# Seven half-width products for the second matmul, and loads that cast, in a two-matmul ReGLU block

## Chip, cores, metric

One core of a Trainium2 chip. The metric is device time in microseconds (us) of one launch. Three executions of the kernel before took 335.81, 336.21 and 337.5 us; the median is 336.21.

## The reference

```python
x  : [16, 256, 512]  -> 4096 rows of 512, float32
w1 : [512, 4096]        w2 : [2048, 512]
h = x @ w1
gate, value = np.split(h, 2, axis=-1)
h = np.maximum(gate, 0) * value
return (h @ w2).astype(np.float32)
```

## The kernel before, in words

All matmuls run in float16 with float32 sums. The 4096 rows are cut into four **stages** (s = 0 to 3) of 1024 rows. A stage has a block phase (the first matmul and the gating) and a second-matmul phase.

**Block phase.** The first matmul is a 2x2 block product. Its row halves are the two groups of 512 rows of the stage, its inner halves the two halves of the 512 columns of x, its column halves gate and value. It is done in seven products instead of eight, on sums of blocks: of x (tiles `x_A11` to `x_A22`, sums `x_S1` to `x_S4`) and of w1 (tiles `w_B11`, `w_B21`, `w_B22` and the sums `w_T1` to `w_T4`). One `Block(jb)` makes 128 gate and 128 value columns; there are 16 in a stage (in stage 0 the blocks 0 and 1 are done plainly, class `Plain`, while w1 still comes in). Each product P1 to P7 of a block is two matmuls of 128x128 by 128x512.

The order is written out by hand in **slots**: block jb places its products at `jb * 7` plus 0, 1, 3, 4, 5, 9, 13 for P1, P5, P2, P6, P3, P7, P4, so that the seven slots of a period are filled by two blocks. Within a block P1 goes to a PSUM bank X, ScalarE copies X to a bank Y (L228), and only then may P2 add to X and P6 to Y. ScalarE also takes W (L235) and Y (L242) out; VectorE makes the gated result `g` with four operations per block (L248, L249, L254, L258).

**Second-matmul phase.** `mm2_stream(s, g)` (L281) yields one matmul at a time: for each of eight 128-row groups it adds up 16 matmuls of 128x128 by 128x512 (L286) in one bank; ScalarE scales the result out (L298), and the sync queue SP stores it. `advance(stream, n)` takes n of them. Ten of them fill free slots at the end of the blocks, four (`TAIL`) the free slots of the next stage's first block.

**Inputs.** w1 comes in as float32 pieces through a staging tile (L195, SP); GpSimd makes the four sums (L203 to L206) and ScalarE three casts (L207). The first 1024 rows of x come in as float32 and are turned by TensorE (L358), later ones are cast by ScalarE (L186) and turned by VectorE in 32x32 blocks (L189). `x_sums` (L158, VectorE) makes S1 to S4. w2 is loaded by GpSimd's queue with a cast (L461).

**Looks.** The kernel also checks that the mean square of each piece of its inputs is in a range, and else runs a general path that is not used here. A look at 1024 columns of w1 or w2 is a squaring with a sum on ScalarE (`look_whole`, L173); the looks at later x are folds on GpSimd (`look`, L164 to L168). `LOOKS` says at which block each is issued, after that block's P6. Before, w1 is looked at in the 16 blocks of stage 1 and w2 in the first 8 blocks of stage 2, one look a block.

All engines' orders are those of the program text (`manual_schedule`); the waits between them are put in by the framework.

Of the kernel before, what the change touches and what calls it, by code (L numbers as in the profile page):

```python
# [16 lines left out]
P = 128  # L17
TH = 512
PERIOD = 7
NWARM = 30  # L20
# [3 lines left out]
SLOT = {"P1": 0, "P5": 1, "P2": 3, "P6": 4, "P3": 5, "P7": 9, "P4": 13}  # L24

# [71 lines left out]
def fast_way(ctx, tc, x2, w1, w2, out2, flag):  # L97

# [4 lines left out]
    NS = T // (2 * TH)  # L109
    NJ = H // P  # L110
    NB = 2 * TH // P
# [3 lines left out]
    xpool = ctx.enter_context(tc.tile_pool(name="xpool", bufs=2))  # L115
    gpool = ctx.enter_context(tc.tile_pool(name="gpool", bufs=1))
    stage = ctx.enter_context(tc.tile_pool(name="stage", bufs=3))
    halfs = ctx.enter_context(tc.tile_pool(name="halfs", bufs=4))
    tmp = ctx.enter_context(tc.tile_pool(name="tmp", bufs=4))
    psx = ctx.enter_context(tc.tile_pool(name="psx", bufs=3, space=bass.MemoryType.PSUM))  # L120
    psy = ctx.enter_context(tc.tile_pool(name="psy", bufs=3, space=bass.MemoryType.PSUM))
    psw = ctx.enter_context(tc.tile_pool(name="psw", bufs=2, space=bass.MemoryType.PSUM))

    x_v = x2.rearrange("(s h tb r) (q c) -> s h q r tb c", h=2, tb=16, r=32, q=4)
    w1_v = w1.rearrange("(p e) (g j) -> p (e g) j", e=4, g=2)
    w2_v = w2.rearrange("(hc p) n -> p hc n", p=P)
    out_v = out2.rearrange("(s b p) n -> s b p n", p=P, b=NB)

    wop = {n: wpool.tile([P, 2, H], F16, name=f"w_{n}") for n in ("B11", "B21", "B22", "T1", "T2", "T3", "T4")}
    w2_sb = wpool.tile([P, NJ, DO], F16, name="w2_sb")
    w_stage = wpool.tile([P, 4, 1024], F32, name="w_stage")
    g_set = {0: gpool.tile([P, NJ, 2 * TH], F16, name="g", tag="g")}

    NX = 8 + (NS - 1) * 32
    st = wpool.tile([P, NX + 16 + NJ // 2], F32, name="st")


# [3 lines left out]
    ident = wpool.tile([P, P], F32, name="ident")  # L143
    for i in range(NWARM):
        pool, nm = (psy, "Y") if i < 16 else (psx, "X")
        t = pool.tile([P, TH], F32, name=nm, tag=nm)
        n = TH if i < 16 else TH // 2
        nc.tensor.matmul(t[:, :n], warm_b[:, :P], warm_b[:, :n], start=True, stop=True)


    def x_tiles():
        return {n: xpool.tile([P, 2, TH], F16, name=f"x_{n}", tag=f"x_{n}")
                for n in ("A11", "A12", "A21", "A22", "S1", "S2", "S3", "S4")}

    def x_sums(o):
        for n, i0, i1, op in (("S1", "A21", "A22", ADD), ("S2", "S1", "A11", SUB), ("S4", "A12", "S2", SUB),
                              ("S3", "A11", "A21", SUB)):
            yield nc.vector.tensor_tensor(o[n], o[i0], o[i1], op=op)  # L158

    def look(t, at):  # L160

        n, m = t.shape[1:]
        fold = tmp.tile([P, n, m], F32, name="fold", tag="fold", bufs=1)
        nc.gpsimd.tensor_tensor(fold, t, t, op=MULT)  # L164
        while m > 2:
            m //= 2
            nc.gpsimd.tensor_tensor(fold[:, :, :m], fold[:, :, :m], fold[:, :, m:2 * m], op=ADD)  # L167
        nc.gpsimd.tensor_tensor(st[:, at:at + n], fold[:, :, 0], fold[:, :, 1], op=ADD)  # L168

    def look_whole(t, at, of, half=False):  # L170

        sq = tmp.tile([P, 1024], F16, name="sq", tag="sq", bufs=1)
        nc.scalar.activation(sq[:, :of], t, SQUARE, scale=(P / of / (2 if half else 1)) ** 0.5,  # L173
                             accum_out=st[:, at:at + 1])

    def load_x(s, i):

        t = stage.tile([P, 8, P], F32, name="xs", tag="xs")
        for q in range(4):
            nc.sync.dma_start(out=t[q * 32:(q + 1) * 32], in_=x_v[s, i // 2, q, :, i % 2 * 8:i % 2 * 8 + 8])  # L180
        return t

    def turn_x(o, t, i):
        ts = slice(i % 2 * 256, i % 2 * 256 + 256)
        c = halfs.tile([P, 8, P], F16, name="xh", tag="xh")
        nc.scalar.copy(out=c, in_=t)  # L186
        halves.append(c)
        for k in range(2):
            nc.vector.transpose(o[f"A{i // 2 + 1}{k + 1}"][:, :, ts].rearrange("p b (tb r) -> p b tb r", r=32),  # L189
                                c.rearrange("p tb (c k b) -> p k b tb c", k=2, b=2)[:, k])  # L190


    def load_w1(eng, jb, n, u):
        t = w_stage[:, u:u + n].rearrange("p u v -> p (u v)").rearrange("p (eg j) -> p eg j", eg=8)
        eng.dma_start(out=t, in_=w1_v[:, :, jb * P:(jb + n) * P])  # L195
        return t.rearrange("p (k b g) j -> p k b g j", k=2, b=2)

    def w1_ops(jb, n, t):

        js = slice(jb * P, (jb + n) * P)  # L200
        b11, b21, b12, b22 = t[:, 0, :, 0], t[:, 1, :, 0], t[:, 0, :, 1], t[:, 1, :, 1]
        op = {n: w[:, :, js] for n, w in wop.items()}
        nc.gpsimd.tensor_tensor(op["T1"], b12, b11, op=SUB)  # L203
        nc.gpsimd.tensor_tensor(op["T2"], b22, (op["T1"]), op=SUB)
        nc.gpsimd.tensor_tensor(op["T3"], b22, b12, op=SUB)
        nc.gpsimd.tensor_tensor(op["T4"], b21, (op["T2"]), op=SUB)  # L206
        return [lambda o=o, i=i: nc.scalar.copy(out=o, in_=i)  # L207
                for o, i in ((op["B11"], b11), (op["B21"], b21), (op["B22"], b22))]

# [4 lines left out]
    class Block:  # L214
# [3 lines left out]
        def mm(self, name, ps, fresh):  # L218
            wn, xn = WX[name]
            for b in range(2):  # L220
                nc.tensor.matmul(ps, wop[wn][:, b, self.jb * P:(self.jb + 1) * P], self.xo[xn][:, b, :],  # L221
                                 start=fresh and b == 0, stop=b == 1, skip_group_check=True)
# [38 lines left out]
    class Plain:  # L261


# [3 lines left out]
        def products(self, h, a1, a2):  # L267
            js = slice(self.jb * P, (self.jb + 1) * P)
            X = psx.tile([P, TH], F32, name="X", tag="X")
            W = psw.tile([P, TH], F32, name="W", tag="W")  # L270
            for a, gate, value in ((a1, "B11", "T3"), (a2, "B21", "B22")):
                for ps, wn in ((X, gate), (W, value)):
                    for b in range(2):
                        nc.tensor.matmul(ps, wop[wn][:, b, js], a[:, b, :], start=a is a1 and b == 0,
                                         stop=a is a2 and b == 1)
            v = tmp.tile([P, 2, TH], F32, name="v", tag="tmp")[:, 0]
            nc.scalar.activation(v, W, COPY, scale=GS)
# [3 lines left out]
    def mm2_stream(s, g):  # L281
        last = s == NS - 1
        for b in range(NB):
            ps = psx.tile([P, DO], F32, name="O", tag="X")
            for hc in range(NJ):
                nc.tensor.matmul(ps, g[:, hc, b * P:(b + 1) * P], w2_sb[:, hc, :],  # L286
                                 start=hc == 0, stop=hc == NJ - 1)
                if hc < NJ - 1:
                    yield
            o = tmp.tile([P, DO], F32, name="o", tag="tmp")  # L290
            if last and b == NB - 1:
                h = DO // 2
                nc.scalar.activation(o[:, :h], ps[:, :h], COPY, scale=1 / GS)  # L293
                nc.scalar.dma_start(out=out_v[s, b, :, :h], in_=o[:, :h])
                nc.vector.tensor_scalar(out=o[:, h:], in0=ps[:, h:], scalar1=1 / GS, scalar2=None, op0=MULT)  # L295
                nc.sync.dma_start(out=out_v[s, b, :, h:], in_=o[:, h:])
            else:
                nc.scalar.activation(o, ps, COPY, scale=1 / GS)  # L298
                nc.sync.dma_start(out=out_v[s, b], in_=o)
            yield  # L300

# [4 lines left out]


    wl = [(0, 1, 0), (1, 1, 1)] + [(jb, 2, jb % 4) for jb in range(2, NJ, 2)]
    ws, copies = {}, []

    def fetch(i, eng):
        if i < len(wl):
            assert not copies
            jb, n, u = wl[i]
            ws[i] = load_w1(eng, jb, n, u)

    def prepare(i):
        jb, n, _ = wl[i]
        copies.extend(w1_ops(jb, n, ws.pop(i)))

    def copy_some(n):
        for c in copies[:n]:
            c()
        del copies[:n]

    def plain_w(i):
        jb, n, _ = wl[i]
        t = ws.pop(i)
        js = slice(jb * P, (jb + n) * P)
        nc.scalar.copy(out=wop["B11"][:, :, js], in_=t[:, 0, :, 0])  # L330
        nc.gpsimd.tensor_copy(out=wop["T3"][:, :, js], in_=t[:, 0, :, 1])
        nc.gpsimd.tensor_copy(out=wop["B21"][:, :, js], in_=t[:, 1, :, 0])
        nc.scalar.copy(out=wop["B22"][:, :, js], in_=t[:, 1, :, 1])

    def plain_w_end(jb, n):
        js = slice(jb * P, (jb + n) * P)
        op = {n: w[:, :, js] for n, w in wop.items()}
        nc.gpsimd.tensor_tensor(op["T1"], op["T3"], op["B11"], op=SUB)
        nc.gpsimd.tensor_tensor(op["T2"], op["B22"], op["T1"], op=SUB)
# [184 lines left out]
```

## Time and profile before

| what | value |
|---|---|
| timed executions | 335.81, 336.21, 337.5 us |
| profiled execution, first to last instruction (span) | 334.7 us |
| median less span, what lies around it | 1.5 us |
| first block product of stages 0, 1, 2, 3 starts at | 20.78, 93.07, 172.74, 251.05 us |
| last matmul starts at | 328.41 us |
| TensorE matmul busy | 321.7 us |
| VectorE, ScalarE, GpSimd busy | 199.5, 180.6, 113.1 us |
| mean granted TensorE clock | 0.997 |

The device time of the profiled execution itself isn't listed; what lies around the span is taken as the 1.5 us above. The starts of the stages are read in the timeline as the first matmul of block 0 (in stage 0 of block 2). A matmul's listed duration is its latency with a modelled end (379 ns for 512 columns); what it costs in a row of matmuls is the distance between starts, 0.216 us.

### The profile page before, as it was taken

Reading aid. Unit: us, or ns where it says so; the run is one execution under the profiler, and the core shown is the slowest. Engines: PE = TensorE matmul, PEld = TensorE weight load, DVE = VectorE, ACT = ScalarE, POOL = GpSimd, SP = SyncE. Lnnn points to the kernel's source line nnn. Section 1 sums busy time; section 2 is a strip of 40 time slices with the busy share of each in tenths; the row PEclk is TensorE's granted clock in tenths of the full one; section 3 lists DMA queues with packets and bytes.
Section 4 is the critical chain, followed back from the end, with each engine's and each line's share of the span. In section 5 each row is a group of like instructions: output and inputs, shape, how many; then the busy total and the mean of one; then the engine's idle time right before and its main releaser. Section 6 shows DMA issues by size and latency. Waiting matters only on the chain. (4 is left out here: it accounts for less than half of the span.)

```text
span 334.7 us, 4222 instructions
## 1 busy us (share of the span) xinstructions
PE 321.7 (96%) x1475; PEld 145.0 (43%) x1475; DVE 199.5 (60%) x307; ACT 180.6 (54%) x332; POOL 113.1 (34%) x142
## 2 busy tenths in 40 slices
PE   8979999999999999999999999999999999999992
PEld 4634444444444444444443444444444444444441
DVE  0477888866038778775207788885805888882000
ACT  2568798832267878764128785554215555541120
POOL 1679979299800000038950000019970000000000
PEclk9999999999999999999999999999999999999998
DMA  8946599942126000004116300004120000000212
GB/s 252 358 144 182 195 238 161 169 113 78 63 90 163 1 0 0 2 1 158 65 63 162 58 2 0 0 2 125 63 96 31 1 1 2 0 0 33 94 65 69
DMA packets 30458, 27.59 MB, mean 82 GB/s; under 512 B 1632, under 2 KB 25440, under 8 KB 30432
## 3 DMA queue, kind: packets, MB, share of 16 engines
q1 hardware_dynamic: 27136, 24.52, 24.8%
q0 software_dynamic: 2112, 2.10, 3.9%
q10 hardware_dynamic: 1184, 0.66, 0.6%
q8 instruction: 13, 0.21, 0.3%
q14 instruction: 13, 0.11, 0.1%
HBM read 20.97 MB, written 8.39 MB: 88 GB/s over the span
## 5 line engine op out<-in xcount | busy, mean ns | idle before, releaser
L286 PE MATMUL O<-w_sb,g 128*128 128x512 f16 x512 | 113.4, 379 | 0.0
L248 DVE SCALAR_TENSOR_TENSOR cc<-W,pu 128x512 f32<-128x512 f32 x62 | 42.9, 692 | 73.3 <-ACT pu L242 73.2
L286 PEld LDWEIGHTS <-g 128*128 128x128 f16 x512 | 50.1, 98 | 60.5 <-issue 0.2
L164 POOL TENSOR_TENSOR fold<-xh 128x1024 f32<-128x1024 f16 x12 | 24.0, 1999 | 114.0 <-ACT xh L186 113.3
L298 ACT ACTIVATE o<-O 128x512 f32<-128x512 f32 x31 | 18.5, 597 | 69.1 <-PE O L286 65.3
L242 ACT ACTIVATE pu<-Y 128x512 f32<-128x512 f32 x62 | 37.0, 597 | 33.6 <-PE Y L221 32.7
L228 ACT COPY Y<-X 128x512 f32<-128x512 f32 x62 | 35.9, 578 | 25.1 <-PE X L221 17.9
L249 DVE SCALAR_TENSOR_TENSOR g<-X,cc 128x512 f16<-128x512 f32 x62 | 42.9, 692 | 2.3
L258 DVE SCALAR_TENSOR_TENSOR g<-Y,cc 128x512 f16<-128x512 f32 x62 | 42.3, 681 | 2.7 <-PE Y L221 2.7
L167 POOL TENSOR_TENSOR fold<-fold 128x512 f32<-128x512 f32 (+2 forms) x72 | 41.3, 574 | 5.6
L254 DVE SCALAR_TENSOR_TENSOR cc<-Y,pu 128x512 f32<-128x512 f32 x62 | 42.3, 682 | 0.1
L235 ACT ACTIVATE pu<-W 128x512 f32<-128x512 f32 x62 | 37.1, 598 | 0.0
L221 PEld LDWEIGHTS <-w_B_89 128*128 128x128 f16 x124 | 12.1, 97 | 23.3 <-issue 12.0
L221 PEld LDWEIGHTS <-w_T_94 128*128 128x128 f16 x124 | 12.1, 97 | 15.8 <-issue 3.5
L221 PEld LDWEIGHTS <-w_T_93 128*128 128x128 f16 x124 | 12.1, 98 | 14.6
L221 PEld LDWEIGHTS <-w_T_91 128*128 128x128 f16 x124 | 12.1, 98 | 14.6
L221 PEld LDWEIGHTS <-w_B_88 128*128 128x128 f16 x124 | 12.0, 97 | 14.7
L221 PEld LDWEIGHTS <-w_T_92 128*128 128x128 f16 x124 | 12.0, 97 | 14.7
L221 PEld LDWEIGHTS <-w_B_90 128*128 128x128 f16 x124 | 12.0, 98 | 14.4
L295 DVE TENSOR_SCALAR o<-O 128x256 f32<-128x256 f32 x1 | 0.4, 425 | 25.3 <-ACT o L293 25.3
L186 ACT CAST xh<-xs 128x1024 f16<-128x1024 f32 x12 | 12.2, 1042 | 5.4 <-DMA xs<-in_x_dram 5.4
L203 POOL TENSOR_TENSOR w_T_91<-w_stage 128x512 f16<-128x512 f32 x7 | 9.2, 1313 | 7.5 <-DMA w_stage<-in_w_dram 7.3
(155 smaller groups left out, 429.9 us busy)
## 6 DMA issues: line engine op xcount, KB each, us to landing
out_dram<-o SPq DMA_DIRECT2D x31, 256.0 KB, 2.0
w_stage<-in_w_dram SPq DMA_DIRECT2D x7, 1024.0 KB, 6.9
xs<-in_x_dram SPq DMA_DIRECT2D x48, 128.0 KB, 3.9
w_sb<-in_w_dram POOLq DMA_DIRECT2D x4, 512.0 KB, 8.6
w_stage<-in_w_dram ACTq DMA_DIRECT2D x1, 512.0 KB, 5.3
w_stage<-in_w_dram SPq DMA_DIRECT2D x1, 512.0 KB, 6.6
x_A_162<-in_x_dram SPq DMA_DIRECT2D x1, 256.0 KB, 2.8
x_A_163<-in_x_dram SPq DMA_DIRECT2D x1, 256.0 KB, 4.1
```

The costliest lines, as they stand in the source:

```text
L164: nc.gpsimd.tensor_tensor(fold, t, t, op=MULT)
L167: nc.gpsimd.tensor_tensor(fold[:, :, :m], fold[:, :, :m], fold[:, :, m:2 * m], op=ADD)
L221: nc.tensor.matmul(ps, wop[wn][:, b, self.jb * P:(self.jb + 1) * P], self.xo[xn][:, b, :], start=fresh and b == 0, stop=b == 1, skip_group ...
L228: nc.scalar.copy(out=self.Y, in_=self.X)
L235: nc.scalar.activation(self.p5, self.W, COPY, scale=GS)
L242: nc.scalar.activation(self.u2, self.Y, COPY, scale=GS)
L248: nc.vector.scalar_tensor_tensor(out=self.c12, in0=self.W, scalar=GS, in1=self.u2, op0=MULT, op1=ADD)
L249: nc.vector.scalar_tensor_tensor(out=self.g[:, self.jb, :TH], in0=self.X, scalar=0.0, in1=self.c12, op0=MAX, op1=MULT)
L254: nc.vector.scalar_tensor_tensor(out=self.c22, in0=self.Y, scalar=GS, in1=self.p5, op0=MULT, op1=ADD)
L258: nc.vector.scalar_tensor_tensor(out=self.g[:, self.jb, TH:], in0=self.Y, scalar=0.0, in1=self.c22, op0=MAX, op1=MULT)
L286: nc.tensor.matmul(ps, g[:, hc, b * P:(b + 1) * P], w2_sb[:, hc, :], start=hc == 0, stop=hc == NJ - 1)
L298: nc.scalar.activation(o, ps, COPY, scale=1 / GS)
```

## The change

- **Second matmul.** The products of g and w2 get the same seven-product scheme: row halves of 512 rows, inner halves of 8 chunks of 128 (`NHC`), column halves of 256 (`HALF`). Per stage and 128-row group b (now 0 to 3) there are seven products of 8 matmuls with 256 columns, so 224 matmuls of 256 columns a stage instead of 128 of 512. `advance` takes 4 at a time where it took 2.
- **Sums of g.** Stages 1 to 3: GpSimd sums S3 block by block for blocks 0 to 7, and S1, S2, S4 for blocks 8 to 13, after each block's P4; VectorE does S1, S2, S4 of the last two (`BY_DVE`). Stage 0: VectorE does all, in eight operations of 2048 columns after the last block.
- **Sums of w2** (`w2_ops`): four GpSimd operations of 2048 columns, issued at block 14 of stage 0.
- **w1 and the first x** are cast by loading DMAs on GpSimd's queue; the ScalarE casts and the staging tile go. `fetch_more` issues the rest of w1, w2 and the casts of later x from there, three fetches each at blocks 2, 4 and 6.
- **Later x** is cast from DRAM to DRAM (`x16`), turned by four transposing DMAs on SP per stage, and read again as rows (`fetch_rows`) for the looks. `xpool` has one buffer where it had two.
- **Looks** at x go to ScalarE, 256 columns each, sixteen a stage; those at w1 to blocks 8 to 15 of stages 1 and 2; those at w2 to blocks 1 to 8 of stage 3.
- 10 warming matmuls where there were 30, and 8 filling ones between the first turn and the first products.

```diff
-    w1_v = w1.rearrange("(p e) (g j) -> p (e g) j", e=4, g=2)
+    w1_v = w1.rearrange("(e p) (g j) -> p e g j", p=P, g=2)
+    def w1_ops(i):
+        turned(lambda n, a, b, o: nc.gpsimd.tensor_tensor(W[n](i), W[a](i), W[b](i), op=o))
+    def w2_ops():
+        turned(lambda n, a, b, o: nc.gpsimd.tensor_tensor(V[n], V[a], V[b], op=o))
...
-    def mm2_stream(s, g):
+    def mm2_stream(s, go):
+        def mm(name, b, ps, fresh):
+            vn, gn = WX[name]
+            for k in range(NHC):
+                nc.tensor.matmul(ps, go[gn][:, k, b * P:(b + 1) * P], V[vn][:, k, :], start=fresh and k == 0,
+                                 stop=k == NHC - 1, skip_group_check=True)
...
+            if name == "P1":
+                d["X"] = take(psx, "X")
+                yield from mm("P1", b, d["X"], True)
+                d["Y"] = take(psy, "Y")
+                nc.scalar.copy(out=d["Y"], in_=d["X"])
...
+        for b in range(0, NB, 2):
+            for name in ("P1", "P2", "P5", "P6", "P3", "P7", "P4"):
+                for c in (b, b + 1):
+                    yield from step(name, c)
...
+    for b in range(0, NB, 2):
+        nc.gpsimd.dma_start(out=xn[:, b:b + 2], in_=x_v[0, :, b:b + 2])
+    fetch_w1(0)
+    make_identity(nc, ident)
+    nc.gpsimd.dma_start(out=xn[:, NB:], in_=x_v[0, :, NB:])
+    for i in range(1, 6):
+        fetch_w1(i)
...
+    for s in range(NS):
+        for i in range(4 * NB):
+            at_block(s, (4 if s == 0 else i // (2 * NB)) + i // 2, lambda s=s, i=i: look_x(s, i))
+    for i in range(2 * NP):
+        at_block(1 + i // NP, 8 + i % NP, lambda i=i: look_w1(i))
+    for i in range(NJ // 2):
+        at_block(3, 1 + i, lambda i=i: look_w2(i))
...
                 if s == 0 and n == "P5" and jb % 2 == 0:
+                    for _ in range(3):
+                        fetch_more(queued)
+                        queued += 1
+                    if jb // 2 + 1 < NP:
+                        w1_ops(jb // 2 + 1)
+                    else:
+                        w2_ops()
+                        w1_ops(0)
                 getattr(blocks[jb], n)()
+                if n == "P1" and s and jb == 4:
+                    xn = fetch_rows(s, 1)
...
+                if n == "P4" and s:
+                    if jb < NHC:
+                        g_sum(nc.gpsimd, go, "S3", jb, jb + 1)
+                    elif jb < NJ - BY_DVE:
+                        for m in ("S1", "S2", "S4"):
+                            g_sum(nc.gpsimd, go, m, jb - NHC, jb - NHC + 1)
...
+        if s == 0:
+            for m in ("S1", "S2", "S4", "S3"):
+                for h in (0, NHC // 2):
+                    g_sum(nc.vector, go, m, h, h + NHC // 2)
+        else:
+            for m in ("S1", "S2", "S4"):
+                g_sum(nc.vector, go, m, NHC - BY_DVE, NHC)
...
+            for h in range(2):
+                for k in range(2):
+                    nc.sync.dma_start_transpose(out=xo[f"A{h + 1}{k + 1}"],
+                                                in_=x16[s + 1][h * TH:(h + 1) * TH, k * 256:k * 256 + 256])
+            xn = fetch_rows(s + 1, 0)
+            advance(stream, 100)
```

## The prediction

> **What bounds the kernel now.** I read the page's engine sums first, then its groups, then the timeline.
>
> ```profile
> PE 321.7 (96%) x1475; PEld 145.0 (43%) x1475; DVE 199.5 (60%) x307; ACT 180.6 (54%) x332; POOL 113.1 (34%) x142
> L286 PE MATMUL O<-w_sb,g 128*128 128x512 f16 x512 | 113.4, 379 | 0.0
> ```
>
> TensorE is busy from end to end, and the second matmul waits for nothing (0.0). So the end is set by TensorE's work plus what it waits for in the blocks. The price of a narrower matmul is in the timeline at the start:
>
> ```profile
> 6.75 1.69 PE L148 MATMUL X<-warm 128*128 128x256 f16 x14
> 8.28 0.72 PE L358 MATMUL W<-ident,x_A_162 128*128 128x128 f32 x4
> ```
>
> 14 matmuls of 256 columns, each with its own weight load, take 8.28 - 6.75 = 1.53 us: 0.1093 us each. Those of L286 start 0.2157 us apart. Weight loads are 0.098 us, so they just hide at 256 columns.
>
> The blocks are bound by a chain through ScalarE (ACT). The timeline of a block of stage 1:
>
> ```profile
> 105.61 0.60 ACT L242 ACTIVATE pu<-Y 128x512 f32<-128x512 f32 x1 [0.59 <-PE Y L221]
> 106.11 1.05 ACT L173 ACTIVATE sq<-w_B_88 128x1024 f16<-128x1024 f16 x1
> 107.06 0.19 ACT L173 ACTIVATION_READ_ACCUMULATOR sq<-w_B_88 128x1 f32 x1
> 107.15 0.59 ACT L228 COPY Y<-X 128x512 f32<-128x512 f32 x1
> 107.66 0.59 ACT L235 ACTIVATE pu<-W 128x512 f32<-128x512 f32 x1
> 108.85 0.60 ACT L242 ACTIVATE pu<-Y 128x512 f32<-128x512 f32 x1 [0.59 <-PE Y L221]
> ...
> 257.81 0.57 ACT L228 COPY Y<-X 128x512 f32<-128x512 f32 x1 [0.70 <-PE X L221]
> ```
>
> See two things. From the copy L228 to the next L242 is 1.70 us, then 0.50 us, then the look (1.04 us), then the next copy: a period of 3.23 us. Without a look (stage 3, last line) ACT idles 0.70 us and the period is 3.03, TensorE's own 14 x 0.2157. So a look has 0.7 to 0.8 us to hide in, and its excess is on the path.
>
> Last, GpSimd (POOL) and VectorE (DVE) together:
>
> ```profile
> 79.67 2.34 POOL L164 TENSOR_TENSOR fold<-xh 128x1024 f32<-128x1024 f16 x1
> 80.17 2.38 DVE L158 TENSOR_TENSOR x_S_788<-x_A_782,x_A_784 128x1024 f16<-128x1024 f16 x1
> 82.08 1.60 POOL L167 TENSOR_TENSOR fold<-fold 128x512 f32<-128x512 f32 x1
> ```
>
> The same sum takes 0.69 us elsewhere. Here it ends at 82.55, 0.54 after GpSimd's operation (82.01), and GpSimd's next one is then late: they take turns, one whole instruction each.
>
> **What the Trainium skill says.** "TensorE: Matmul & The Clock Gate", Back-to-back issue gap: N/2.4 + 2.5 ns, so 109 and 216 ns; the trace agrees. Its Part 1 says that about 3.4 us of idleness halves the clock; the warming matmuls agree from the other side (0.427 us apart at first, 0.216 later). "SBUF — State Buffer", Who interferes with whom: a VectorE instruction with two SBUF inputs and a GpSimd instruction that reads SBUF exclude each other; the lines above agree. "DMA: Bandwidth & Descriptors", Latency and other measured facts: transposing DMAs reach 261 GB/s; nothing in this trace shows one.
>
> **The change, part by part.** The reckoning is against the profiled span, 334.7 us; the median is 1.5 above it, which I add at the end.
>
> *Second matmul.* 512 x 0.2157 = 110.4 us becomes 4 x 224 x 0.1093 = 97.9: **-12.5 us**, 3.1 a stage, all on the path. Its copies: P1's X to Y (256 columns, about 0.37 us by the 384 ns of L293) lies under the other group's 8 matmuls (0.87 us); that cover is thin (0.2 us) but is not taken by other work. P4 waits likewise for a VectorE operation of 0.43 us (L295). I cost both at nothing, at most 0.2 us x 32 = 6.
>
> *Start.* The first block product starts at 20.78. GpSimd's casting loads (L461: 0.76 us to issue, first packet 1.65 us after the issue, 4.2 MB in 11.9 us, so 2.97 us a MB) bring half of x by 5.7, the first w1 by 9, the rest of x by 12, the next w1 pair by 15. Turning in float16, two plain blocks (6.9 us) and the copies between give a first block at 18.9: -1.9. In stage 0 ACT's casts go (periods of 3.65, 3.66 and 3.3 shrink towards 3.05), -1.5.
>
> *GpSimd in stage 0.* Its queue does not wait for TensorE, only for data and itself: 15 issues x 0.76 end at 12.9; from 15.3 (data) on 7 x 4.65 for `w1_ops` (L338 to L341: 1.16 each) and 11 issues x 0.76 = 8.4. So `w2_ops` starts at 56.3. Blocks 6 and 8 wait 0.8 us for their sums meanwhile. A sum of w2 has 2048 columns: 0.2 us plus 2048 x 1.87 ns (from 1.16 at 512 and L168's 0.2) is 4.0 us; the four end at 60, 64, 68, 72, then `w1_ops(0)` to 77. The DRAM-to-DRAM issues aren't shown; 0.5 to 2 us each (three), I take 0.76.
>
> *End of stage 0.* With these, the last P4 is at t = 65.4 (before: 68.04). VectorE then owes eight sums of 2048 columns, 1.1 us each (0.54 for 1024 once let in). From 66.7 they take turns with GpSimd's remaining operations (4.0, 4.0, then four of 1.15): S1 is whole at 74.3, S2 78.8, S4 83.3, S3 85.6. TensorE wants S1 at 67.1 (12 x 0.1093 after P4) and each next 16 matmuls (1.75 us) later, so it follows: P7 at 85.7. Then 136 matmuls to stage 1's first block: 14.9 us, so 100.6, plus about 2 because a wait of 7 us lets the clock fall: **102.6 against 93.07, +9.5**. Without the turns it would be 90.7.
>
> *Looks.* A look of 256 columns is 0.31 + 0.09 = 0.40 us (from 0.95 at 1024 and 0.52 at 512). Two in a block, 0.80, fit in. One at w, 1.04, costs 0.2 as before. Both together: 1.70 + 0.49 + 1.84 = 4.03, so +1.0. That is block 8 of stages 1 and 2, and blocks 1, 2, 3, 5, 6, 7, 8 of stage 3: 7 x 1.0 there, where ACT had no look before.
>
> *Stages 1 to 3.* 224 x (0.2157 + 0.1093) = 72.8 us of work. Waits: 0.4 at the first block (as shown before), 1.0 + 7 x 0.2 for looks, 0.4 for S1 of the last two blocks (P4's result, then 0.69 us on VectorE). Stage 1: 76.0 (was 79.67), stage 2: 76.0 (78.31). Stage 3 to the last matmul: 72.8 + 0.4 + 7.0 + 0.2 + 0.4 = 80.8 (77.57). Sum -3.7 - 2.3 + 3.2 = **-2.8**. GpSimd's sums of g (six blocks x 3 x 1.14 = 20.5 us beside 3.03 to 3.23 a block) end within a microsecond of the last P4, just not late; VectorE's block operations have one SBUF input and share nothing.
>
> *Later x.* The ACT casts and VectorE turns lay under the second matmul: nothing saved. The four transposing DMAs stand on SP ahead of `fetch_rows` and of the output stores. They wait for the last block to free its x tiles (one buffer now). By the skill's 261 GB/s they take 1 us each; they have some 15 us before VectorE's sums fall late, so up to about 4 us each costs nothing, 8 us each some 10 us a stage. I take nothing. The stores behind them have four result tiles.
>
> *Tail.* Narrower last pieces: -0.2.
>
> Sum: 334.7 + 9.5 - 2.8 - 0.2 = 341.2; with 1.5 around it, **342.7, say 342.5**.
>
> **Rivals.**
> A, faster. GpSimd gets through `w2_ops` before VectorE starts on g, so no turns are taken at the end of stage 0. It decides at about 66: the queue would have to start `w2_ops` by 50 instead of 56 for half the loss to go, and by 46 for all. Then 93.07 becomes 90.7, and 334.7 - 2.4 - 2.8 - 0.2 + 1.5 = 331. For it: the GpSimd price at 2048 columns is extrapolated. Against: 41 us of issues and sums stand ahead, each with a row.
> B, much slower. Loads are the bound at first: w1 rows arrive as 512-byte pieces, cast issues are dearer, or transposes are slow. 4 us later data for the first sums plus 1.2 us on each of three unseen issues is +7.6, all along GpSimd's chain: 350. Slow transposes would give more.
> C. The gain in TensorE doesn't come because weight loads of 0.098 us under 0.109 us no longer hide when operands differ: 0.12 a matmul would add 10 us. The warming row speaks against it.
> A failing look would start the general path and cost hundreds of us; every column is still written, so I give it nothing.
>
> **How the numbers follow.** Turns at the end of stage 0: 0.56, likeliest, own range 337 to 348 (`w2_ops` from 52 to 60 moves it by -4 to +4). A: 0.17 at 331. Between A and that: 0.10 at 336. B and C: 0.17 at 350 and up. A difference of 0.5% (1.7 us) is about what can be told from none. Faster by more: A and a little, 0.19. Same, 334.5 to 337.9: 0.11. Slower: 0.70. The range 331 to 351 leaves out a fifth, mostly above.
>
> **What would show it.** L286's successor with 896 matmuls 0.109 us apart; TensorE idle 7 us before the first P5 of stage 0's second matmul and some 4 before the next two, with VectorE sums of over 4 us beside GpSimd ones; block periods of 4.0 us in stage 3, blocks 1 to 8; nothing waiting for the transposes. The prediction is wrong if stage 1 starts before 95, if stage 3's periods stay at 3.2, or if TensorE waits for x between stages.

## The result, and the profile after

The changed kernel takes **344.95 us** (median of four, 344.56 to 345.75) against 336.11 us (335.81 to 337.5, four) before: a ratio of **1.0262, 95% interval 1.0237 to 1.0286**. It is slower by 8.8 us. The profiled execution has a span of 343.8 us and took 345.75 us itself, 0.8 above the median.

| point in the trace, us | before | predicted | after |
|---|---|---|---|
| first block product, stage 0 | 20.78 | 18.9 | 20.03 |
| stage 1 starts | 93.07 | 102.6 | 101.01 |
| length of stage 1, of stage 2 | 79.67, 78.31 | 76.0, 76.0 | 76.39, 76.39 |
| stage 3 to the last matmul | 77.36 | 80.8 | 84.39 |
| last matmul to the end of the span | 6.2 | 6.0 | 5.7 |

The page after, first the engine sums, then the groups of the second matmul (the last two columns: busy and mean, then idle time before them and who ended it):

```profile
PE 311.8 (91%) x1847; PEld 179.8 (52%) x1847; DVE 216.0 (63%) x328; ACT 191.3 (56%) x451; POOL 166.4 (48%) x146
...
L270 PE MATMUL X<-w_sb,g 128*128 128x256 f16 x256 | 30.6, 273 | 0.0
...
L270 PE MATMUL W<-v_T,g_S 128*128 128x256 f16 x128 | 16.7, 287 | 6.0 <-DVE g_S L261 6.0
```

TensorE is busy for 10 us less, and its share fell from 96% to 91%: the products got cheaper and the time went into waits. The products that read g itself wait for nothing, as before (0.0). Those that read `g_S`, the sums of g, wait for VectorE.

The first place where this happens is the end of stage 0. The timeline of GpSimd there (start, duration), with its last two sums of w2 and the first of its small sums of w1:

```profile
65.76 4.07 POOL L153 TENSOR_TENSOR v_T<-w_sb 128x2048 f16<-128x2048 f16 x1
69.78 5.04 POOL L153 TENSOR_TENSOR v_T<-w_sb,v_T 128x2048 f16<-128x2048 f16 x1
74.78 2.12 POOL L150 TENSOR_TENSOR wt<-wr 128x512 f16<-128x512 f16 x1
76.98 2.02 POOL L150 TENSOR_TENSOR wt<-wr,wt 128x512 f16<-128x512 f16 x1
```

and of VectorE beside it (two sums to a line):

```profile
68.70 7.19 DVE L261 TENSOR_TENSOR g_S<-g 128x2048 f16<-128x2048 f16 x2
75.82 4.26 DVE L261 TENSOR_TENSOR g_S<-g_S,g 128x2048 f16<-128x2048 f16 x2
80.00 4.26 DVE L261 TENSOR_TENSOR g_S<-g,g_S 128x2048 f16<-128x2048 f16 x2
84.19 2.35 DVE L261 TENSOR_TENSOR g_S<-g 128x2048 f16<-128x2048 f16 x2
```

Read the last line first: once GpSimd has ended (83.2), two sums take 2.35 us. Beside GpSimd the first two take 7.19. The two engines take turns, one whole instruction each. GpSimd's fourth sum is listed with 5.04 us, 1 us more than the others, because VectorE's first sum ran ahead of it. VectorE's second ended at 75.89, 1.07 us after that fourth sum (74.82), about the time that such a sum takes alone. The middle pairs and GpSimd's small sums alternate in the same way, and both show about 2.1 us an instruction, their own time and the other's. TensorE follows S1, S2 and S4 (S3, not shown, comes last); it begins with the first half of a sum, so each appears as 4 and 12 matmuls:

```profile
67.90 1.47 PE L270 MATMUL X<-w_sb,g 128*128 128x256 f16 x12
70.97 0.61 PE L270 MATMUL W<-v_T,g_S 128*128 128x256 f16 x4 [1.59 <-DVE g_S L261]
75.95 2.74 PE L270 MATMUL W<-v_T,g_S 128*128 128x256 f16 x12 [4.38 <-DVE g_S L261]
78.48 1.06 PE L270 MATMUL Y<-v_T,g_S 128*128 128x256 f16 x4
80.14 2.25 PE L270 MATMUL Y<-v_T,g_S 128*128 128x256 f16 x12 [0.59 <-DVE g_S L261]
```

Twelve matmuls take 1.47 us; after the idle stretch they take 2.74, so about 0.21 apart: the lower clock that "TensorE: Matmul & The Clock Gate", Part 1, lets one expect after idleness. The trace agrees: its granted clock is 0.50 between 75.0 and 81.7 us, and 1.00 before and after.

The second place is stage 3. ScalarE's timeline of block 1, whose period is 4.31 us:

```profile
259.56 0.60 ACT L217 ACTIVATE pu<-Y 128x512 f32<-128x512 f32 x1 [0.59 <-PE Y L196]
260.05 0.41 ACT L183 ACTIVATE sq<-xn 128x256 f16<-128x256 f16 x1
260.36 0.19 ACT L183 ACTIVATION_READ_ACCUMULATOR sq<-xn 128x1 f32 x1
260.58 0.42 ACT L183 ACTIVATE sq<-xn 128x256 f16<-128x256 f16 x1
260.90 0.19 ACT L183 ACTIVATION_READ_ACCUMULATOR sq<-xn 128x1 f32 x1
261.12 1.06 ACT L183 ACTIVATE sq<-w_sb 128x1024 f16<-128x1024 f16 x1
262.09 0.19 ACT L183 ACTIVATION_READ_ACCUMULATOR sq<-w_sb 128x1 f32 x1
262.18 0.58 ACT L203 COPY Y<-X 128x512 f32<-128x512 f32 x1
```

From the first look to the copy that lets TensorE go on it is 2.13 us. From start to start, a copy follows an accumulator read by 0.09 us, but a look follows it by 0.22, twice here. TensorE waits for that copy before its P2:

```profile
262.81 0.59 PE L196 MATMUL X<-x_A,wr 128*128 128x512 f16 x2 [1.13 <-ACT Y L203]
```

Such waits are 8.1 us in stage 3, against 2.9 in the whole run of the kernel before. The third place, small, is the judgement in block 13 of stage 3. There VectorE compares the 88 results of the looks with two limits, and TensorE and VectorE make one flag of it:

```profile
305.22 0.20 DVE L399 TENSOR_SCALAR ok<-st 128x88 f32<-128x88 f32 x1
305.45 1.11 DVE L400 SCALAR_TENSOR_TENSOR ok<-st,ok 128x88 f32<-128x88 f32 x1
```

The second comparison has as few elements as the first and takes five times as long. What VectorE owes behind it comes late, and TensorE waits 0.68 us for the flag.

### The profile page after: what moved, and what is told of

Same layout as the page of the kernel before. It is cut to its first block, busy times and chain, and to the rows that moved or that the text cites. A ratio compares the mean times of both kernels' runs of the same rounds, so it can differ in the third digit from the quotient of the medians.

```text
span 343.8 us, 5094 instructions
## 1 busy us (share of the span) xinstructions
PE 311.8 (91%) x1847; PEld 179.8 (52%) x1847; DVE 216.0 (63%) x328; ACT 191.3 (56%) x451; POOL 166.4 (48%) x146
## 4 chain that ended last, share of the span: by engine, by line
PE 62%; ACT 13%; DVE 8%; issue 7%; POOL 6%; DMA 3%; ACTq 0%; DVEq 0%; POOLq 0%
PE Y L196 16%; PE X L196 13%; PE Y L270 11%; PE X L270 8%; PE W L196 8%; PE W L270 7%; ACT sq L183 6%; DVE g_S L261 5%; ACT Y L203 4%; POOL wt L150 3%; DMA wr<-in_w_dram 3%; ACT pu L217 2%; POOL wr L337 2%; DVE cc L223 1%; POOL w_sb L431 1%
## 5 line engine op out<-in xcount | busy, mean ns | idle before, releaser
L261 POOL TENSOR_TENSOR g_S<-g 128x512 f16<-128x512 f16 x42 | 48.5, 1155 | 141.7 <-DVE g L233 141.7
L196 PE MATMUL X<-x_A,wr 128*128 128x512 f16 x248 | 73.6, 378 | 11.8 <-ACT Y L203 11.1
L196 PEld LDWEIGHTS <-wt 128*128 128x128 f16 x496 | 48.0, 97 | 59.5 <-POOL wt L150 2.5
L196 PE MATMUL Y<-x_S,wt 128*128 128x512 f16 x248 | 73.7, 379 | 0.0
L196 PEld LDWEIGHTS <-wr 128*128 128x128 f16 x372 | 36.1, 97 | 60.9 <-issue 24.6
L270 PEld LDWEIGHTS <-g_S 128*128 128x128 f16 x512 | 50.7, 100 | 16.9 <-DVE g_S L261 10.0
L196 PE MATMUL W<-x_S,wr 128*128 128x512 f16 x124 | 36.9, 379 | 0.8 <-DVE x_S L178 0.8
L196 PE MATMUL W<-x_S,wt 128*128 128x512 f16 x124 | 36.9, 380 | 0.7 <-POOL wt L150 0.7
L196 PE MATMUL Y<-x_A,wt 128*128 128x512 f16 x124 | 36.9, 379 | 0.7 <-DVE flag L409 0.7
L270 PE MATMUL Y<-v_T,g_S 128*128 128x256 f16 x256 | 32.1, 279 | 0.9 <-DVE g_S L261 0.9
```

What stands on the lines that cost most here:

```text
L196: nc.tensor.matmul(ps, W[wn](self.jb // 2)[:, b, js], self.xo[xn][:, b, :], start=fresh and b == 0, stop=b == 1, skip_group_check=True)
L261: eng.tensor_tensor(go[n][:, h0:h1], go[i0][:, h0:h1], go[i1][:, h0:h1], op=op)
L270: nc.tensor.matmul(ps, go[gn][:, k, b * P:(b + 1) * P], V[vn][:, k, :], start=fresh and k == 0, stop=k == NHC - 1, skip_group_check=True)
```

## The experiments

Each is an edit to the changed kernel, and each ratio is to the kernel before on the same chip. That kernel's medians lie between 335.93 and 336.13 us there, so the runs can be compared with each other. A second measure inside a trace is the time from the last P4 of stage 0 to the start of stage 1: 25.03 us before, 33.54 after.

**Who is late at the end of stage 0.** The first run leaves out GpSimd's sums of w2; the products that need them read blocks of w2 in their place:

```diff
-         **{n: t for n, t in v_t.items()}}
+         "T1": w2_sb[:, :NHC, HALF:], "T2": w2_sb[:, NHC:, HALF:], ...}
...
-                        w2_ops()
                         w1_ops(0)
```

> Leaves out the four GpSimd sums of w2 (quarters of w2 itself are used in their place), so GpSimd is done at about 62 us, before VectorE starts its eight sums of g in stage 0. Theory of the turns (the two engines exclude each other instruction by instruction): the eight sums run at 1.1 us each from 68.7, all done at 77.6 instead of 86.5; TensorE's first P7 of the second matmul at 77.7, stage 1 starts at 91 to 92 instead of 101.0, total about 335.5. Rival (TensorE waits for VectorE's own eight sums, in line after the last block, whatever GpSimd does): at most 1 us is gained, stage 1 at 99 or later, total 343 or more.

Measured: 336.73 us, ratio 1.0022 (1.001 to 1.0033). VectorE's timeline of this run:

```profile
68.46 2.35 DVE L260 TENSOR_TENSOR g_S<-g 128x2048 f16<-128x2048 f16 x2
```

The same pair takes 2.35 us instead of 7.19, and stage 1 starts at 92.10, 24.88 us after the last P4. That is 8.2 us back in the whole time. Still, 24.88 is hardly less than the 25.03 of the kernel before: even without turns the products gain almost nothing in stage 0, because TensorE waits 2.2 us for VectorE's sums. And the run takes away two things at once, GpSimd's work beside VectorE and the sums of w2 that matmuls might wait for. The next one parts them: GpSimd makes the same sums at the same place, and nobody reads them.

```diff
-         **{n: t for n, t in v_t.items()}}
+         "T1": w2_sb[:, :NHC, HALF:], "T2": w2_sb[:, NHC:, HALF:], ...}
+    VT = {**V, **v_t}
...
-        turned(lambda n, a, b, o: nc.gpsimd.tensor_tensor(V[n], V[a], V[b], op=o))
+        turned(lambda n, a, b, o: nc.gpsimd.tensor_tensor(VT[n], VT[a], VT[b], op=o))
```

> The changed kernel with GpSimd's four sums of w2 where they were, but read by nobody: the second matmul reads blocks of w2 in place of its four sums, so the result leaves these sums out and no matmul waits for them. Theory (GpSimd's and VectorE's operations take turns at the end of stage 0): nothing changes, 345.0, stage 1 starts at about 101, VectorE's sums of g take 4 us and more while GpSimd's run. Rival: TensorE is late because the sums of w2 themselves are late; then it goes to the value without them, 336.7, and stage 1 starts at about 92.

Measured: 345.47 us, ratio 1.0271 (1.0236 to 1.0307), stage 1 at 100.18. VectorE again:

```profile
67.87 7.20 DVE L262 TENSOR_TENSOR g_S<-g 128x2048 f16<-128x2048 f16 x2
```

The pair takes 7.20 us again. So it is GpSimd's operations beside VectorE's that cost, not the sums being late. The third way is to have no sums of g in stage 0. `mm2_plain` is the second matmul as it was before, with 16 matmuls of 512 columns a bank:

```diff
-        stream = mm2_stream(s, go)
+        plain_now = s == 0
+        stream = mm2_plain(s, g) if plain_now else mm2_stream(s, go)
...
-        if s == 0:
-            for m in ("S1", "S2", "S4", "S3"):
-                for h in (0, NHC // 2):
-                    g_sum(nc.vector, go, m, h, h + NHC // 2)
-        else:
+        if not plain_now:
```

> Stage 0's second matmul as before (128 matmuls of 512 columns, no sums of g there); everything else as in the changed kernel, GpSimd's sums of w2 included. Theory: nothing waits at the end of stage 0, stage 1 starts 25 us after the last block product (67.7), at 92.7 instead of 101.0: 8.3 us less, total about 336.6. Rival (the wait there is small change and the seven products pay even in stage 0): 3.1 us more, 348.

Measured: 337.04 us, ratio 1.0027 (1.0012 to 1.0042), stage 1 at 91.75, 25.04 after the last P4. TensorE does the 3.1 us more of work and ends earlier all the same.

**What the products are worth, and what the rest costs.** The second matmul plain in all stages (`plain_now = True`, no sums of g or w2 anywhere):

> Second matmul of 512-column matmuls in all four stages, no sums of g or w2; loads, casts, turns of x and looks as in the changed kernel. Theory: stage 0 gains 8.3 us as in the run with stage 0 alone plain, stages 1 to 3 lose 3.1 us each, total about 346 (9.3 above that run). Rival (the seven products gain nothing because of hidden waits in each stage): equal to the run with stage 0 alone plain, about 336.6.

Measured: 346.15 us, ratio 1.03 (1.0282 to 1.0317). This gives the ledger. Without its seven products the change costs 10.0 us (346.15 - 336.11), and 9.5 of these lie in stage 3, 86.84 us to the last matmul against 77.36, where the looks at x and at w2 meet. The products in stages 1 to 3 bring 9.1 (to 337.04): 3.2 and 3.3 in stages 1 and 2, 2.4 in stage 3. Those in stage 0 then lose 7.9 (to 344.95).

Stage 3 gains less because of the judgement. In this run GpSimd has no sums of g to make, and the same second comparison is short:

```profile
303.24 0.25 DVE L419 SCALAR_TENSOR_TENSOR ok<-st,ok 128x88 f32<-128x88 f32 x1
```

It takes 0.25 us in place of 1.11, and block 13 takes 3.22 in place of 4.07. So the long comparison is one more meeting with GpSimd.

**Looks on ScalarE.** The eight looks at w2 go from stage 3's blocks into the second matmul of stages 1 and 2, two after each pair of P7:

```diff
-    for i in range(NJ // 2):
-        at_block(3, 1 + i, lambda i=i: look_w2(i))
+    LATE = {}
+    for i in range(NJ // 2):
+        LATE.setdefault((1 + i // 4, i // 2 % 2), []).append(lambda i=i: look_w2(i))
...
+                if b % 2:                        # behind the P7 of a pair
+                    for f in LATE.get((s, b // 2), ()):
+                        f()
```

> Only moves the eight looks at w2 from blocks 1 to 8 of stage 3 into the second-matmul phases of stages 1 and 2, two after each P7 pair. Theory (ScalarE's chain copy-P2-P6-look sets the block period): the seven periods of 4.31 in stage 3 fall to 3.13 and block 4's to 3.03, 8.5 us less, and the second-matmul phases take no longer since ScalarE waits there; total about 336.5. Rival one (GpSimd's new sums slow the blocks of stage 3): no gain. Rival two (ScalarE is near its limit in the second-matmul phases too): half of it comes back there, total 340 to 341.

Measured: 336.35 us, ratio 1.0013 (1.0001 to 1.0026). Stage 3 falls from 84.39 to 75.92 us and stages 1 and 2 keep their 76.38: beside the second matmul these looks are free.

**The gap between looks, and the judgement.**

```diff
-        sq = tmp.tile([P, 1024], F16, name="sq", tag="sq", bufs=1)
+        if of == 256 and at % 2:
+            sq = tmp.tile([P, 256], F16, name="sq2", tag="sq2", bufs=1)
+        else:
+            sq = tmp.tile([P, 1024], F16, name="sq", tag="sq", bufs=1)
...
-        nc.vector.tensor_scalar(out=ok, in0=st, scalar1=HIGH, scalar2=None, op0=LE)
-        nc.vector.scalar_tensor_tensor(out=ok, in0=st, scalar=LOW, in1=ok, op0=GE, op1=MULT)
+        nc.vector.tensor_scalar(out=ok[:, :n], in0=st, scalar1=HIGH, scalar2=None, op0=LE)
+        nc.vector.tensor_scalar(out=ok[:, n:], in0=st, scalar1=LOW, scalar2=None, op0=GE)
```

> The changed kernel with two small edits that bear on stages 1 to 3. (1) Looks of 256 columns alternate between two scratch tiles, where all wrote one. (2) The judgement's second comparison reads one operand in SBUF, where it read two. Theory: a second look starts 0.22 us after the first one's accumulator read, where 0.09 is usual, because both write the one scratch tile; so two looks at x cost a period of 3.03 instead of 3.13 and three looks 4.03 to 4.18 instead of 4.31, together 2.0 in stages 1 and 2 and 2.0 in stage 3; the 0.8 of stage 0 is not passed on, since GpSimd's queue sets its end. The judgement's operation falls from 1.1 us to 0.2 and block 13 of stage 3 from 4.07 to about 3.05, 1.0. Sum: 345.0 - 5.0 = 340.0. Rival: the gap between looks is ScalarE's own after an accumulator read; then periods stay at 3.13 and 4.31 and only the judgement's 1.0 goes, 344.0.

Measured: 341.3 us (340.48 to 342.54), ratio 1.0152 (1.0113 to 1.0191). The first edit, the second scratch tile, did what it should. ScalarE's timeline of block 1 of stage 3:

```profile
257.55 0.41 ACT L186 ACTIVATE sq<-xn 128x256 f16<-128x256 f16 x1
257.86 0.19 ACT L186 ACTIVATION_READ_ACCUMULATOR sq<-xn 128x1 f32 x1
257.95 0.40 ACT L186 ACTIVATE sq<-xn 128x256 f16<-128x256 f16 x1
```

It is 0.09 us to the next look, so the gap came from the shared tile and not from the accumulator read. Behind the first block of a stage, blocks with two looks take 3.01 to 3.06 us, those with three 4.02 to 4.06; stages 1 and 2 are 0.9 shorter each, stage 3 2.1. The second edit, in the judgement, did nothing: block 13 still has 4.12 us. VectorE's lines there,

```profile
300.71 0.19 DVE L402 TENSOR_SCALAR ok<-st 128x88 f16<-128x88 f32 x1
300.82 1.19 DVE L403 TENSOR_SCALAR ok<-st 128x88 f16<-128x88 f32 x1
```

and GpSimd's:

```profile
300.80 1.15 POOL L264 TENSOR_TENSOR g_S<-g,g_S 128x512 f16<-128x512 f16 x1
```

The first comparison came between two of GpSimd's sums. The second waited for the one that had just started, and ended at 302.01, 0.06 us after it. I had counted SBUF inputs only. "SBUF — State Buffer", Who interferes with whom, also names `tensor_scalar`, which can run in a mode that uses the shared pair with one input; these lines agree.

**Transposing DMAs, doubled.** Each is issued twice (`for k in (0, 0, 1, 1)` in place of `range(2)`).

> The changed kernel with each transposing DMA issued twice (eight a stage instead of four, the same data into the same tiles). Theory: they are hidden. SP is held 1.25 us by each, so 5 us more at the end of each stage's block phase, and the last lands about 5 us later, still before VectorE's sums of x would make the next stage late; the output stores behind them have four result tiles. So within 0.3% of the changed kernel: 345.0, at most 346. Rival: SP or the transposes are close to the path, because the stores of the second matmul stand behind them and the result tiles run out; then some 3 to 5 us a stage on three stages, 354 to 360.

Measured: 360.94 us, ratio 1.074 (1.0699 to 1.0781). My expectation was wrong. The rival had the right cause but too small a size: it gave 3 to 5 us to each of three stages. The sync queue in the changed kernel at the end of stage 1:

```profile
151.84 6.93 SPq L490 DMA_TRANSPOSE x_A<-x  x4
...
162.39 1.23 SPq L301 DMA_DIRECT2D out_dram<-o  x2
```

and in this run:

```profile
151.10 20.48 SPq L490 DMA_TRANSPOSE x_A<-x  x8
...
172.29 0.93 SPq L301 DMA_DIRECT2D out_dram<-o  x2
```

Twice as many held SP three times as long. The issues themselves take 1.23 to 1.30 us in the changed kernel and 1.23 to 1.72 here. The rest is waiting, 1.8 us in the changed kernel (before the third) and 10.1 here. The repeats write the same tiles, and each goes out 0.02 us after the transfer that it repeats has landed (155.83 after 155.81, for one). So this run tests a longer hold of the queue rather than twice the transposing. Then in this run ScalarE, and behind it TensorE:

```profile
177.18 0.38 ACT L293 ACTIVATE o<-X 128x256 f32<-128x256 f32 x1 [9.52 <-DMA out_dram<-o]
```

```profile
178.53 3.57 PE L270 MATMUL W<-w_sb,g_S 128*128 128x256 f16 x16 [6.08 <-ACT pv L289]
```

The first pair's stores came 10 us late, the four result tiles were all taken, and ScalarE waited for one. Stages 1 and 2 became 8.4 and 8.2 us longer: in stage 1, 6.08 of TensorE's waiting and 2.2 from the lower clock after it (32 matmuls take 5.67 us where 3.50 is usual). VectorE's sums of x ran at 173.5 instead of 164.8, and no wait of TensorE is put down to them. In stage 0 the same holding cost nothing: SP was free at 83.1, and the first store, late because of VectorE's turns, was due at 86.2.

**What paid, together.** Stage 0 plain, the looks at w1 and w2 in the second-matmul phases, two scratch tiles, and the judgement with one-operand comparisons. The part of the edit that no run above has:

```diff
+    LATE = {}
     for i in range(2 * NP):
-        at_block(1 + i // NP, 8 + i % NP, lambda i=i: look_w1(i))
+        LATE.setdefault((0, i // 2) if i < 14 else (1, 0), []).append(lambda i=i: look_w1(i))
     for i in range(NJ // 2):
-        at_block(3, 1 + i, lambda i=i: look_w2(i))
+        LATE.setdefault((1 + i // 4, i // 2 % 2), []).append(lambda i=i: look_w2(i))
```

> A version that keeps what paid. Stage 0's second matmul is plain (512 columns, no sums of g there), as in the run that measured 337.0. The sixteen looks at w1 go into the second-matmul phases of stage 0 (14, two after each 16 matmuls) and of stage 1 (2), the eight at w2 into those of stages 1 and 2, where ScalarE idles. Two scratch tiles for the looks and the one-operand judgement as in the other run. Theory: from 337.0, stages 1 and 2 lose 1.3 at block 8 and 7 x 0.2 behind it plus 7 x 0.1 before it, 3.4 each less what is left over; stage 3 loses 7 x 1.28 + 0.2 = 9.2; stage 0 0.8; the judgement 1.0. 337.0 - 6.2 - 9.2 - 0.8 - 1.0 = 319.8, so 318 to 322. Rival: GpSimd's sums of g (3.42 us a block for six blocks) become the bound when blocks take 3.03 us, and the looks that moved delay the copies of the second matmul; then each stage gives back 1 to 2 us: 323 to 326.

Measured: **321.24 us, ratio 0.9556 (0.953 to 0.9582)**, better than both kernels. The engine sums of its page:

```profile
PE 306.8 (96%) x1751; PEld 169.5 (53%) x1751; DVE 200.7 (63%) x312; ACT 186.7 (59%) x439; POOL 164.4 (52%) x146
```

TensorE is at 96% again, now of a shorter span. All periods of stages 1 to 3 but the first of each and the judgement's (4.10) are 3.00 to 3.06, so GpSimd's sums of g, the rival's bound, hold nothing up. Of the 1.4 us missing to 319.8, 1.0 is the judgement's, whose gain the run before had already refuted. Last, the judgement moved to where GpSimd must wait for VectorE:

```diff
-        LOOKS[3, 14] = [lambda: count(fit, P * 2 * n)]
+        LOOKS[3, 11] = [lambda: count(fit, P * 2 * n)]
...
-    at_block(3, 13, judge)
...
+                if (s, jb, n) == (3, 9, "P3"):
+                    judge()
```

> The combined version, with the judgement moved from P6 of block 13 to behind P3 of block 9 in stage 3, and the flag's matmul to block 11. There GpSimd has ended its sum of block 7 and waits for VectorE's P4 of block 8, which stands behind the judgement, so nothing of GpSimd runs beside it. Theory (the comparisons wait for a GpSimd sum to end, whichever operands they read): both comparisons take 0.2 us, no period of stage 3 is above 3.4, and the time is 0.7 to 1.0 below the combined version: 320.4. Rival: the second comparison costs 1.1 us by itself, or the flag's matmul makes TensorE wait wherever it stands; then a period of about 4.1 shows up at block 9, 10 or 11 and the time stays at 321.2.

Measured: 320.97 us, ratio 0.9545 (0.9531 to 0.956), against 0.9556: no difference that can be told. The comparisons themselves became short:

```profile
269.60 0.19 DVE L426 TENSOR_SCALAR ok<-st 128x88 f16<-128x88 f32 x1
269.71 0.20 DVE L427 TENSOR_SCALAR ok<-st 128x88 f16<-128x88 f32 x1
```

But the judgement is still 0.6 us more for VectorE in a period that has 0.4 to spare, and periods of 3.66 and 3.22 follow, where I had expected none above 3.4. The mechanism is confirmed: the same two comparisons are short where no GpSimd sum runs beside them. The gain that I wrote down (0.7 to 1.0) was too high; stage 3 is 0.3 us shorter.

## Why the prediction was right, point by point

- **The sign and the main cause** came out: 342.5 predicted, 344.95 measured. VectorE and GpSimd taking turns at the end of stage 0 cost 7.9 and 8.2 us by the two runs that take the turns away. The look clash of stage 3, second in the prediction, cost about as much: 8.6 us by the run that moves the looks at w2.
- **The size is partly luck.** The end of stage 0 came 1.6 us cheaper than reckoned, stages 1 to 3 4.6 dearer, the tail 0.4 cheaper. What lies around the span is 1.8 to 1.9 us in every run whose profile lists both, not 1.5.
- **Second matmul, -12.5.** Right where it can be seen: 0.109 us a matmul, and 3.2 and 3.3 us in stages 1 and 2 against 3.1. Stage 3 got 2.4, since the sums of g that come with the products made the judgement dearer. Rival C is out. In stage 0 the gain lies under the wait.
- **GpSimd in stage 0.** `w2_ops` started at 57.58 (predicted 56.3), its sums took 4.07 (4.0). Rival A would have needed 50. Its 331 was too low as well: the run without turns in stage 0 took 336.73, since the dearer stage 3 stayed and stage 1 started at 92.10 and not at 90.7.
- **End of stage 0.** S1, S2, S4, S3 were whole at 75.9, 80.1, 84.3 and 86.5 against 74.3, 78.8, 83.3 and 85.6; stage 1 started at 101.01 against 102.6. The term that was mis-sized is the 2 us for the clock. The slow matmuls are there, but they fall into time in which TensorE would have waited for the next sum. (Where no later wait hides them they do cost: 2.2 us in the run with doubled transposes.) The idle stretches are shorter than the 7 us and twice some 4 that the prediction named: 1.59 and 4.38 before the two halves of the first P5, then 0.59, 1.48 and 0.35.
- **Start, -1.9.** Measured -0.75, since the first half of x had landed at 8.33 instead of 5.7. It is not a fixed number: in the other runs, whose start is the same code, the first block product came between 18.38 and 20.86.
- **Blocks of stage 0, -1.5 and +0.8 for the waits for w1's sums.** From the first block product to the last P4 it is 47.44 us against 47.26, so +0.2. The waits for GpSimd's sums came (periods of 3.39 and 3.73), but the first period stayed at 3.64, and seven blocks take 3.13 because of two looks at x. The last P4 came at 67.47 instead of 65.4. By the trace this cost nothing: GpSimd's third sum of w2 ran until 69.82, and VectorE's first sum would have had to wait for it at 66.7 too.
- **Looks.** The step that failed in size is "1.70 + 0.49 + 1.84 = 4.03". Three looks take 2.13 us, since a look that follows a look pays 0.13 more. That is 7 x 0.28 = 2.0 us in stage 3, and a period of 3.13 instead of 3.03 with two looks. The run with two scratch tiles shows the 4.03.
- **Stages 1 to 3.** -2.8 predicted, +1.8 measured (-3.3 - 1.9 + 7.0; the prediction took 77.57 for stage 3 before, 0.2 too much). Stages 1 and 2 were 0.4 longer than predicted, stage 3 3.6: 2.0 from the looks, 1.0 from the judgement, which I had not priced at all, the rest not traced one by one. The S1 wait of the last blocks, 0.4, isn't there.
- **Later x, nothing.** Right for the kernel as it is: nobody waits for the transposes. The estimate of 1 us each from 261 GB/s fits the distance at which a pair lands (0.83 to 1.10 us), but an issue holds SP for 1.23 to 1.35 us and a transfer takes 3.4 to 4.8 to land. The margin was misread. I put it at 4 us each because of VectorE's sums of x; what gives way first is the store queue behind them, by its four result tiles, which the prediction named and did not price. At the end of stage 1 SP has 3.0 us to spare (159.40 to the first store at 162.39), and a hold of 20.48 us in all cost 8 us a stage.
- **Tail, -0.2.** It was -0.6.

## What to carry to other kernels

Before giving GpSimd or VectorE a long elementwise operation, look at what the other does at that time, and count `tensor_scalar` between SBUF tiles among the operations that must take turns; what a new product saves on TensorE can be lost at one such meeting. Put work that may be done at any time, like the looks here, where its engine idles and not in the phase whose chain runs through it. And when transfers are put ahead of others on a queue, ask how many buffers the others have, not only who reads the new data.

## What the runs showed that I had not expected

- A ScalarE squaring with a sum that writes the same tile as the one before starts 0.22 us after the accumulator read; with another tile 0.09.
- A comparison of 128x88 by `tensor_scalar` takes 0.2 us alone and 1.19 when a GpSimd sum has just started; one with two SBUF inputs takes 0.25 and 1.11.
- A transposing DMA of 512x256 takes 1.23 to 1.35 us to issue; a repeat into the same tile is not issued before the first has landed, and all that stands behind it on the queue waits too.
- In the changed kernel the casting loads' later issues on GpSimd waited up to 1.79 us for earlier loads to land, so fifteen issues ended at 17.4 us instead of the 12.9 that 0.76 each had led me to.
- Sums that one engine makes after the last block can take back all that a cheaper product brings: in stage 0 the seven products without turns take 24.88 us from the last P4 to the next stage, the plain ones 25.04.
